# Differential attention on one core: the second map's weights scaled and added by one VectorE operation per unit, instead of two GpSimd operations

## The chip, the core and the metric

The kernel runs on one core of a Trainium2 chip. The metric is the device time of one execution in microseconds (us); the time of before is the median of three runs. The engines have short names in the profile: PE is TensorE (PEld is its loading of weights), DVE is VectorE, ACT is ScalarE, POOL is GpSimd, SP is the engine that issues the DMAs.

## The reference

Two layers over 1024 tokens of width 1024: multi-head latent attention, then differential attention with a bias by distance. In the second layer every head has two softmax maps, and what multiplies the values is their weighted difference:

```python
sc = jnp.einsum('bqhcd,bkhcd->bhcqk', qb, k).astype(jnp.float32)
bias = -slopes[None, :, None, None, None] * dist[:, None, None]
p = jax.nn.softmax(sc + bias, axis=-1)
a = p[:, :, 0] - lam * p[:, :, 1]
return jnp.einsum('bhqk,bkhd->bqhd', a.astype(v.dtype), v)
```

All in float32; 8 heads of two 64-wide halves, 8 blocks of 128 queries each.

## The kernel before

The second layer's attention is cut into 64 units (`Unit1`), one for each head and block of 128 queries. Matrix products in float32 are made of three products of rounded parts (a high part `hi` and a remainder `lo`), so every operand is split in two before it is used.

One pass of the loop over `u` (from -1 to 64) starts unit `u + 1` and finishes unit `u`. All five engines run in the order in which the loop records their instructions; nothing is reordered in this part. What one pass does:

- PE: the scores of unit `u + 1` for both maps (L1277, 12 matmuls into two PSUM tiles `S`), the transposes of unit `u`'s combined weights `p` (L818, 8 of them into two PSUM tiles `T`), then 24 or 48 matmuls of a projection of the layer (L1155 to L1157, or L1148 to L1150 for `W` blocks), and in every odd pass the product of two units' weights with the values (L1312). In every even pass the output of that product is transposed (L1318), which takes a `T` tile too. When a head is complete, its normalised output is transposed in two `T` tiles (L1346, in the passes u = 13, 21, 29, 37, 45, 53 and 61; called a closing below).
- DVE: the maximum of map 0 and of map 1 (L1283, each with a small L1285 behind it), a remainder of the last projection block, the reciprocal and the ratio `l1` (L1295, L1296), the remainder of the split of the transposed weights (L826, twice), up to four steps of a head's normalisation (L1332, L113, L115, L117, and L1336, which scales 128x128 pieces of the output `o`), and the rounding of the next weight block (L99).
- ACT: the two exponentials (L1291), which leave the sums of their rows, the rounding of the transposed weights (L97), copies.
- POOL: the weighted sum of the two maps (`combine`, L1303 and L1304), and the remainder of the next weight block (L104, `wbl`).

`T` tiles are two, used in turn: a new transpose can only be written when the tile's last readers, L97 on ACT and L826 on DVE, are done. In the passes u = 48, 51, 54 and 57 (`DOUBLE`) two units are started, the second one behind the split. Pages of SBUF (`page`) come from one pool of 49.

Of the kernel before, what the change touches and what calls it, by code (L numbers as in the profile page):

```python
# [12 lines left out]
ALU = mybir.AluOpType  # L13
# [42 lines left out]
def body(tc, x, c, positions, ada_w, ada_b, norm_g, mla_w_in, mla_q_norm_g, mla_w_q_up,  # L56
# [4 lines left out]
    with ctx:  # L61
# [30 lines left out]
        V, A, G, T = nc.vector, nc.scalar, nc.gpsimd, nc.tensor  # L92
# [1167 lines left out]
        class Unit1:  # L1260
# [36 lines left out]

            def combine(self):
                p0, p1 = self.p
                if self.u in (0,):  # L1300
                    V.scalar_tensor_tensor(p0, p1, self.l1, p0, op0=ALU.mult, op1=ALU.add)
                else:
                    G.tensor_scalar(p1, p1, self.l1, 1.0, op0=ALU.mult, op1=ALU.mult)  # L1303
                    G.tensor_tensor(p0, p0, p1, op=ALU.add)  # L1304
                self.p = p0

        def pv1(acc, h, ch):
# [255 lines left out]
```

## Time and profile before

| | before |
|---|---|
| median of 3 runs | 1655.2 us (1653.62 to 1655.92) |
| profiled execution | 1657.92 us, span 1656.1 us |
| PE busy | 1541.9 us (93%) |
| DVE busy | 1192.3 us (72%) |
| ACT busy | 814.3 us (49%) |
| POOL busy | 752.8 us (45%) |
| mean granted TensorE clock | 0.978 |

The profiled execution is 1.8 us longer than its span (what lies around the first and the last instruction) and 2.7 us longer than the median. Busy times are sums over the whole kernel, whose stages have different limits: the latent attention lies at about 260 to 690 us, the differential attention at about 890 to 1530 us. A PE that reads as busy is not PE at its peak, since matmuls are pipelined and their ends are modelled.

### The profile page before, as it was taken

Reading aid. Unit: us, or ns where it says so; the run is one execution under the profiler, and the core shown is the slowest. Engines: PE = TensorE matmul, PEld = TensorE weight load, DVE = VectorE, ACT = ScalarE, POOL = GpSimd, SP = SyncE. Lnnn points to the kernel's source line nnn. Section 1 sums busy time; section 2 is a strip of 40 time slices with the busy share of each in tenths; the row PEclk is TensorE's granted clock in tenths of the full one; section 3 lists DMA queues with packets and bytes.
Section 4 is the critical chain, followed back from the end, with each engine's and each line's share of the span. In section 5 each row is a group of like instructions: output and inputs, shape, how many; then the busy total and the mean of one; then the engine's idle time right before and its main releaser. Section 6 shows DMA issues by size and latency. Waiting matters only on the chain. (4 is left out here: it accounts for less than half of the span.)

```text
span 1656.1 us, 24862 instructions
## 1 busy us (share of the span) xinstructions
PE 1541.9 (93%) x9111; PEld 1315.9 (79%) x9111; DVE 1192.3 (72%) x2189; ACT 814.3 (49%) x1614; POOL 752.8 (45%) x612
## 2 busy tenths in 40 slices
PE   4788999999999999999999999899999999999797
PEld 3787778888888888888787898788777887777686
DVE  6766666888888888885536558686867676766764
ACT  6422125776777777785223444444444444445411
POOL 4444472443453453573353544554545354544422
PEclk8899999999999999999999999999999999999899
DMA  9007662110211111211224122423141313125122
GB/s 365 20 14 239 205 212 78 40 40 15 64 34 47 51 40 52 81 62 39 102 89 153 64 90 77 153 77 106 61 128 64 103 51 128 53 89 191 64 73 92
DMA packets 91585, 153.31 MB, mean 93 GB/s; under 512 B 5872, under 2 KB 60230, under 8 KB 91464
## 3 DMA queue, kind: packets, MB, share of 16 engines
q1 hardware_dynamic: 91464, 151.73, 27.3%
q8 instruction: 72, 1.18, 0.3%
q14 instruction: 49, 0.40, 0.1%
HBM read 126.01 MB, written 25.17 MB: 91 GB/s over the span
## 5 line engine op out<-in xcount | busy, mean ns | idle before, releaser
L826 DVE TENSOR_TENSOR ptl<-T,pth 128x512 fp32r<-128x512 f32 x384 | 246.7, 684 | 48.1 <-ACT pth L97 43.8
L97 ACT ACTIVATE pth<-T 128x512 fp32r<-128x512 f32 x384 | 207.4, 591 | 93.0 <-PE T L818 87.9
L1283 DVE CUSTOM_DVE_ANT_0 p<-S,dist 128x1024 f32<-128x1024 f32 x128 | 156.2, 1220 | 130.7 <-PE S L1277 87.6
L1291 ACT ACTIVATE p<-p,m 128x1024 f32<-128x1024 f32 x128 | 147.5, 1153 | 157.0 <-DVE m L1285 141.1
L818 PE MATMUL T<-ident,p 128*128 128x128 f32 x1536 | 205.8, 276 | 12.9 <-POOL p L1304 5.5
L854 POOL TENSOR_SCALAR p<-p,l 128x1024 f32<-128x1024 f32 x128 | 144.2, 1126 | 152.0 <-DVE l L853 104.5
L818 PEld LDWEIGHTS T<-ident,p 128*128 128x128 f32 x1536 | 170.9, 141 | 50.8 <-POOL p L1304 15.8
L1303 POOL TENSOR_SCALAR p<-p,l 128x1024 f32<-128x1024 f32 x63 | 71.2, 1130 | 299.9 <-ACT pth L97 290.9
L1155 PE MATMUL A<-hT,wbh 128*128 128x512 f32 x416 | 167.4, 402 | 0.0
L1156 PE MATMUL A<-hT,wbh 128*128 128x512 f32 x416 | 163.2, 392 | 2.9 <-DVE hT L104 2.9
L1157 PE MATMUL A<-hT,wbl 128*128 128x512 f32 x416 | 162.8, 391 | 0.0
L1304 POOL TENSOR_TENSOR p<-p,p 128x1024 f32<-128x1024 f32 x63 | 158.4, 2515 | 5.3
L847 DVE TENSOR_REDUCE m<-S 128x1 f32<-128x1024 f32 x128 | 155.9, 1218 | 2.1 <-PE S L843 0.3
L852 ACT ACTIVATE p<-S,m 128x1024 f32<-128x1024 f32 x128 | 143.2, 1118 | 15.8 <-DVE m L847 10.4
L1277 PE MATMUL S<-KK,QQ 64*128 64x512 f32 x768 | 108.2, 408 | 5.1 <-DVE m L1283 5.1
L841 PE MATMUL S<-Kh,Q 96*128 96x512 f32 x256 | 108.4, 424 | 4.5 <-ACT p L852 2.6
L888 POOL TENSOR_TENSOR og<-ot,og 64x256 f32<-64x256 f32 x64 | 53.1, 830 | 130.6 <-DVE ot L887 128.5
L842 PE MATMUL S<-Kl,Q 96*128 96x512 f32 x256 | 100.4, 392 | 0.0
L843 PE MATMUL S<-Kh,Q 96*128 96x512 f32 x256 | 100.4, 392 | 0.0
L104 POOL TENSOR_TENSOR wbl<-wblk,wbh 128x1024 fp32r<-128x1024 f32 x32 | 78.0, 2440 | 36.9 <-issue 20.9
L1156 PEld LDWEIGHTS A<-hT,wbh 128*128 128x128 f32 x416 | 78.7, 189 | 18.6 <-DVE hT L104 3.7
L1155 PEld LDWEIGHTS A<-hT,wbh 128*128 128x128 f32 x416 | 78.6, 189 | 17.1 <-issue 1.3
(329 smaller groups left out, 3667.2 us busy)
## 6 DMA issues: line engine op xcount, KB each, us to landing
dist<-DD SPq DMA_DIRECT2D x64, 512.0 KB
adaw<-in_ada_w_dram SPq DMA_DIRECT2D x48, 512.0 KB
wblk<-in_diff_w_in_dram SPq DMA_DIRECT2D x32, 512.0 KB
qraw<-in_mla_w_q_up_dram SPq DMA_DIRECT2D x16, 288.0 KB
x<-in_x_dram SPq DMA_DIRECT2D x8, 512.0 KB
wraw<-in_mla_w_in_dram SPq DMA_DIRECT2D x8, 512.0 KB
OGD<-gt SPq DMA_DIRECT2D x8, 512.0 KB
Q<-RD SPq DMA_DIRECT2D x64, 64.0 KB
```

The source lines that it names most:

```text
L97: A.activation(o, i, AF.Copy)
L818: T.transpose(tp[:, i * P:(i + 1) * P], p[:, kt * P:(kt + 1) * P], ident)
L826: V.tensor_tensor(ptl[n][:, :, o], src, f(pth[n][:, :, o]), op=ALU.subtract)
L847: V.tensor_reduce(self.m, self.ps, axis=AX.XY, op=ALU.max, negate=True)
L852: A.activation(p.rearrange("p (a b) -> p a b", b=512), self.ps, AF.Exp, bias=self.m, accum_out=l)
L854: G.tensor_scalar(p, p, l, 1.0, op0=ALU.mult, op1=ALU.mult)
L1155: T.matmul(ps, w[0][:, k], a, start=k == 0, stop=False)
L1156: T.matmul(ps, w[0][:, k], b, start=False, stop=False)
L1157: T.matmul(ps, w[1][:, k], a, start=False, stop=k == 7)
L1283: V.tensor_tensor_reduce(out=p, in0=self.ps[c_].rearrange("p a b -> p (a b)"), in1=dist[self.u], op0=ALU.subtract, op1=ALU.max, scale=1.0, ...
L1291: A.activation(p, p, AF.Exp, bias=self.m[c_], scale=2.0 ** -(self.h + 1), accum_out=L0[self.h][:, self.qt:self.qt + 1] if c_ == 0 else sel ...
L1304: G.tensor_tensor(p0, p0, p1, op=ALU.add)
```

## The change

`combine` had two forms: for unit 0 one DVE instruction that multiplies `p1` by the column `l1` and adds `p0`, for the other 63 units two POOL instructions (scale `p1` in place, then add it to `p0`). The change uses the first form for all units.

```diff
             def combine(self):
                 p0, p1 = self.p
-                if self.u in (0,):
-                    V.scalar_tensor_tensor(p0, p1, self.l1, p0, op0=ALU.mult, op1=ALU.add)
-                else:
-                    G.tensor_scalar(p1, p1, self.l1, 1.0, op0=ALU.mult, op1=ALU.mult)
-                    G.tensor_tensor(p0, p0, p1, op=ALU.add)
+                V.scalar_tensor_tensor(p0, p1, self.l1, p0, op0=ALU.mult, op1=ALU.add)
                 self.p = p0
```

The orders of PE, ACT and SP stay what they were. From L1301 on the changed file's lines are numbered 4 lower.

DVE in the pass u = 21, a closing (the time 1116 to 1125 us in the trace of before): `S` are the scores, `l` is `l1`, `ptl` the remainder of the transposed weights, `o` the head's output. Before:

```order
L1283 ISA p_11469,m_2170_11468<-S_11438,dist_11230 128x1024
L1283 ISA m_2170_11468 128x1
L1285 TENSOR_SCALAR m_2170_11468<-m_2170_11468 128x1
L1174 SCALAR_TENSOR_TENSOR QQ_11451<-A_11395,QQ_11451 128x512
L1295 RECIPROCAL l_2172_11472<-l_2172_11472 128x1
L1296 SCALAR_TENSOR_TENSOR l_2172_11472<-l_2052_10832,nlam,l_2172_11472 128x1
L826 TENSOR_TENSOR ptl_11388<-T_11458,pth_11387 128x4x128
L826 TENSOR_TENSOR ptl_11392<-T_11463,pth_11391 128x4x128
L1336 TENSOR_SCALAR o_9970<-o_9970,ory_11099 128x128 x4
```

And now, at the same place:

```order
L1283 ISA p_11448,m_2170_11447<-S_11417,dist_11211 128x1024
L1283 ISA m_2170_11447 128x1
L1285 TENSOR_SCALAR m_2170_11447<-m_2170_11447 128x1
L1174 SCALAR_TENSOR_TENSOR QQ_11430<-A_11374,QQ_11430 128x512
L1295 RECIPROCAL l_2172_11451<-l_2172_11451 128x1
L1296 SCALAR_TENSOR_TENSOR l_2172_11451<-l_2052_10817,nlam,l_2172_11451 128x1
L1300 SCALAR_TENSOR_TENSOR p_11433<-p_11448,l_2172_11451,p_11433 128x1024
L826 TENSOR_TENSOR ptl_11367<-T_11437,pth_11366 128x4x128
L826 TENSOR_TENSOR ptl_11371<-T_11442,pth_11370 128x4x128
L1332 TENSOR_SCALAR o_9963<-o_9963,ory_11081 128x128 x4
```

The new instruction for unit 22 (L1300) stands between the ratio and the two splits of unit 21 (L826), so the splits and everything behind them on DVE come after it; L1336 of before is L1332 now.

POOL over the passes around u = 16 to 20, where `wbl` is the remainder of a weight block. Before:

```order
L1303 TENSOR_SCALAR p_11057<-p_11057,l_2096_11060 128x1024
L1304 TENSOR_TENSOR p_11042<-p_11042,p_11057 128x1024
L104 TENSOR_TENSOR wbl_11105<-wblk_10935,wbh_11104 128x1024
L1303 TENSOR_SCALAR p_11174<-p_11174,l_2118_11177 128x1024
L1304 TENSOR_TENSOR p_11159<-p_11159,p_11174 128x1024
L1303 TENSOR_SCALAR p_11263<-p_11263,l_2135_11266 128x1024
L1304 TENSOR_TENSOR p_11248<-p_11248,p_11263 128x1024
L104 TENSOR_TENSOR wbl_11307<-wblk_11135,wbh_11306 128x1024
L104 TENSOR_TENSOR wbl_11311<-wblk_11137,wbh_11310 128x1024
```

And now:

```order
L104 TENSOR_TENSOR wbl_11087<-wblk_10919,wbh_11086 128x1024
L104 TENSOR_TENSOR wbl_11287<-wblk_11117,wbh_11286 128x1024
L104 TENSOR_TENSOR wbl_11291<-wblk_11119,wbh_11290 128x1024
```

Of POOL's work in this stage only the remainders of weight blocks are left.

## Rows read from the trace of the kernel before

**Rows 1.** Busy time of each engine in the stretch of the differential attention: us from the span's start, its length, busy us and instructions of each engine, then granted clock, DMA share and GB/s.

```profile
890.00:1530.00 640.00, 614.32 (x3821) 512.24 (x3819) 445.73 (x910) 294.79 (x630) 299.86 (x155) 0.99 0.29 95
```

**Rows 2.** The waits of PE, of its weight loads and of DVE in the same stretch: who waited for whom, us in total, times, the longest.

```profile
PE T L1346 <- DVE o L1336: 12.1, 9, 2.0
PE T L818 <- POOL p L1304: 5.5, 6, 1.2
PE S L1277 <- DVE m L1283: 5.1, 8, 0.9
...
PEld T L818 <- POOL p L1304: 15.8, 23, 1.6
...
DVE p L1283 <- PE S L1277: 87.6, 34, 5.6
```

**Rows 3.** POOL's groups of instructions in the same stretch: shapes and count, busy us, mean ns of one, then the idle time before them.

```profile
L1304 POOL TENSOR_TENSOR p<-p,p 128x1024 f32<-128x1024 f32 x63 | 158.4, 2515 | 5.3
L1303 POOL TENSOR_SCALAR p<-p,l 128x1024 f32<-128x1024 f32 x63 | 71.2, 1130 | 299.9 <-ACT pth L97 290.9 <-DVE l L1296 2.4 <-PE T L1185 2.2
L104 POOL TENSOR_TENSOR wbl<-wblk,wbh 128x1024 fp32r<-128x1024 f32 x29 | 70.5, 2434 | 36.2 <-issue 20.9 <-DVE wbh L99 10.8 <-PE A L1312 4.5
```

**Rows 4.** DVE's groups in the same stretch, in the same form.

```profile
L1336 DVE TENSOR_SCALAR o<-o,ory 128x128 f32<-128x128 f32 x48 | 25.1, 584 | 0.2
...
L113 DVE TENSOR_TENSOR ort<-ory 128x8 f32<-128x8 f32 x19 | 18.3, 963 | 0.4
L117 DVE SCALAR_TENSOR_TENSOR ory<-ort,ory 128x8 f32<-128x8 f32 x19 | 16.9, 888 | 0.7
...
L1332 DVE SCALAR_TENSOR_TENSOR oms<-oms,oss 128x8 f32<-128x8 f32 x7 | 13.9, 1984 | 0.2
L115 DVE SCALAR_TENSOR_TENSOR ort<-ort,oms 128x8 f32<-128x8 f32 x19 | 12.0, 629 | 0.5
```

**Rows 5.** Two of these lines over the whole kernel: shortest, median and longest duration in ns, first and last start.

```profile
L1336 DVE TENSOR_SCALAR o<-o,ory x64: 273/279/2429, 1030.6 to 1580.0; 128x128 f32<-128x128 f32 x64
...
L1332 DVE SCALAR_TENSOR_TENSOR oms<-oms,oss x8: 166/2278/2307, 998.0 to 1576.2; 128x8 f32<-128x8 f32 x8
```

**Rows 6.** A closing, u = 21, in order of time for DVE, POOL and PE: start us, duration us, engine, line, count, and in brackets the idle time before with its releaser.

```profile
1120.94 1.29 DVE L826 TENSOR_TENSOR ptl<-T,pth 128x512 fp32r<-128x512 f32 x2
1122.14 2.96 DVE L1336 TENSOR_SCALAR o<-o,ory 128x128 f32<-128x128 f32 x4
...
1122.29 2.34 POOL L1304 TENSOR_TENSOR p<-p,p 128x1024 f32<-128x1024 f32 x1
...
1121.68 0.66 PE L1346 MATMUL T<-ident,o 128*128 128x128 f32 x4 [0.17 <-DVE ptl L826]
1122.57 0.30 PE L1346 MATMUL T<-ident,o 128*128 128x128 f32 x1 [0.23 <-DVE o L1336]
1124.77 0.90 PE L1346 MATMUL T<-ident,o 128*128 128x128 f32 x3 [1.90 <-DVE o L1336]
1125.32 3.27 PE L1312 MATMUL A<-pth,V 128*128 128x256 f32 x16
```

**Rows 7.** Four stretches of 4 us behind closings, in the columns of rows 1.

```profile
1124.00:1128.00 4.00, 3.23 (x16) 3.21 (x17) 2.40 (x5) 0.00 (x0) 0.63 (x1) 0.57 0.19 80
1208.00:1212.00 4.00, 2.69 (x13) 2.57 (x14) 3.49 (x6) 0.00 (x0) 1.55 (x2) 0.72 0.09 35
...
1376.00:1380.00 4.00, 2.97 (x14) 2.94 (x15) 3.26 (x6) 0.00 (x0) 1.50 (x2) 0.63 0.13 55
...
1468.00:1472.00 4.00, 3.86 (x21) 3.75 (x22) 2.27 (x6) 0.00 (x0) 1.59 (x2) 0.65 0.46 148
```

**Rows 8.** Unit 0's combination, the one that DVE makes already, with what stands around it on DVE.

```profile
899.32 0.22 DVE L1296 SCALAR_TENSOR_TENSOR l<-l,nlam,l 128x1 f32<-128x1 f32 x1
899.58 1.28 DVE L1301 SCALAR_TENSOR_TENSOR p<-p,l,p 128x1024 f32<-128x1024 f32 x1
900.78 0.68 DVE L99 CAST wbh<-wblk 128x1024 fp32r<-128x1024 f32 x1
```

**Rows 9.** Splits (for one of them with the ratio ahead of it) and output transposes of three even passes, DVE's rows and then PE's: the first of the stage, the one with the widest and the one with the narrowest distance.

```profile
928.99 1.29 DVE L826 TENSOR_TENSOR ptl<-T,pth 128x512 fp32r<-128x512 f32 x2
...
987.57 0.22 DVE L1296 SCALAR_TENSOR_TENSOR l<-l,nlam,l 128x1 f32<-128x1 f32 x1
987.86 1.29 DVE L826 TENSOR_TENSOR ptl<-T,pth 128x512 fp32r<-128x512 f32 x2
1110.77 1.29 DVE L826 TENSOR_TENSOR ptl<-T,pth 128x512 fp32r<-128x512 f32 x2
...
930.68 0.38 PE L1318 MATMUL T<-ident,ot 128*128 128x128 f32 x2
989.90 0.38 PE L1318 MATMUL T<-ident,ot 128*128 128x128 f32 x2
1112.18 0.38 PE L1318 MATMUL T<-ident,ot 128*128 128x128 f32 x2
```

**Rows 10.** The pass with two weight-block remainders that came closest to the next ratio: DVE's rounding, POOL's remainders, DVE's next ratio.

```profile
1104.90 1.29 DVE L99 CAST wbh<-wblk 128x1024 fp32r<-128x1024 f32 x2
...
1105.66 5.14 POOL L104 TENSOR_TENSOR wbl<-wblk,wbh 128x1024 fp32r<-128x1024 f32 x2 [1.11 <-DVE wbh L99]
...
1110.41 0.41 DVE L1296 SCALAR_TENSOR_TENSOR l<-l,nlam,l 128x1 f32<-128x1 f32 x1
```

## The prediction, made before the changed kernel was run

> **What bounds the kernel now.** I read the busy times of the whole span first (the table above: PE 93%, DVE 72%, POOL 45%), then those of the stretch in which the change lies, 890 to 1530 us: PE is busy 614.3 of 640 us, DVE 445.7, POOL 299.9 [rows 1]. So this stage is PE's, and all that the change can give back directly are PE's 25.7 idle us and the time that PE spends at a lower clock. Next the waits of PE in that stretch [rows 2]: 12.1 us at the closings of heads (L1346 waits for the scaled pieces of `o`, L1336), 5.5 us at the transposes L818 for POOL's L1304, 5.1 us at the second scores of the passes that start two units. The weight loads show the second of these as 15.8 us in 23 waits, but most of that lies beside a matmul that is still running.
>
> Then I asked why L1336 is late. It takes 273 ns at its shortest and 279 in the middle, yet 2429 at its longest [rows 5], and in the closing at 1122 us four of them take 2.96 us: the group starts at 1122.14, POOL's L1304 runs from 1122.29 to 1124.63, and PE goes on at 1124.77 [rows 6]. The tiny steps of the normalisation do the same: L1332 works on 8 columns, takes 166 ns at its best and 2278 in the middle [rows 5]. So a DVE instruction that meets a running L1304 stands still until it ends. Busy time minus count times the undisturbed duration (0.279 for L1336, 0.17 for the others) is 11.7 us for L1336, 15.1 for L113, 13.7 for L117, 12.7 for L1332 and 8.8 for L115, together 62 us of DVE that reads as busy and is standing still [rows 4].
>
> The Trainium skill has a rule for this, on the page "SBUF — State Buffer", section "Who interferes with whom": VectorE and GpSimd share a pair of ports as an exclusive lock, which a VectorE instruction needs in a two-port mode, or with two SBUF inputs against a GpSimd instruction that reads SBUF, and who comes second is held for the whole of the other. The standstills agree with it. By that rule the instruction that the change adds can be held in the same way, by what POOL still does; its price is in rival 2.
>
> **The change, part by part.** Removed: 63 times L1303 and L1304, 229.6 us of POOL [rows 3]. That in itself is worth nothing, since POOL is idle half the stage. Added: 63 DVE instructions of the form that unit 0 uses already: 1.28 us, with the next one starting 1.20 us after it [rows 8]. DVE in the stage goes from 445.7 to 445.7 + 63 x 1.28 - up to 62, some 465 us of 625: 74%, still not the bound. Five things then move PE, (a) to (e).
>
> On the Trainium skill's page "Perfetto Trace Analysis", section "Optimizing Scalar/DVE Operations", one finds that work of a saturated VectorE may be handed to other engines, even to GpSimd; the change does the opposite. If DVE were the bound here, the time would be that of rival 3 in place of the sum below; 445.7 of 640 us speaks against it, and the page itself adds that the shared port can undo such a move.
>
> (a) The transposes no longer wait for POOL. The weights were ready 3.6 us behind the ratio (1.13 + 2.5 [rows 3]), now 1.24 us. In the passes where they waited, the scores stand between, 1.6 us of PE work. The gain is 5.5 us by PE's row; it counts only what lies behind the modelled end of the matmul before. The loads' row, 15.8, counts what lies beside that matmul too, and is the upper bound. PE's row is the nearer; I take 7, a little above it.
>
> (b) The closings. Six lie in the stage. There, L1336 would find POOL idle. Between the second split and the last piece there then remain four times some 0.22 us, and L1346 of the second tile must follow these; on the other side the splits come 1.17 us later, which the pass before gives back, since its own standstill of about 2.1 us [rows 5] is gone too. I put the rest at 0.5 us a closing, between 0.3 (only the pieces) and 1.4 (the whole of the late split besides): 12.1 - 6 x 0.5 = 9 us gained, between 3.7 and 10.3.
>
> (c) The clock. Behind four of the six closings the granted clock falls from 1.00 to between 0.57 and 0.72 over 4 us, behind a wait of PE of 1.9 us [rows 6, 7]; in part of these stretches PE runs at 1.2 GHz in place of 2.4. The matmuls of L1312 then take 3.27 us for 16. Time lost: 4 us x (0.43 + 0.28 + 0.37 + 0.35) = 5.7 us. PE's waits of 1.2 us at L818 [rows 2] have no such dip behind them in any slice I read. If a closing costs 0.5 us, all four dips go: 5.7 us; if it keeps 1.4, perhaps none.
>
> (d) The price. L826 starts 1.17 us later in each pass (the new instruction starts 0.04 us behind the ratio's end and occupies 1.20 [rows 8]; L826 started 0.07 behind it, as at 987.57 + 0.22 to 987.86 [rows 9]). The transposes of `p` hold both `T` tiles until L826 has read them. In even passes L1318 is the next to want one. From the end of the first L826 (0.68 us after the pair's start) to L1318 there are 1.01 us in the first such pass, 1.36 in the widest and 0.73 in the narrowest; read the same way, 20 of the 27 lie between 0.9 and 1.15, and three more passes, with a transpose of values there instead, at 1.0 to 1.1 [rows 9]. From a release to PE's start it takes 0.06 us (1120.94 + 0.68 to 1121.68 in [rows 6]). So PE stands 1.17 + 0.06 - 1.01 = 0.22 us where it did not, nothing in the widest, 0.50 in the narrowest: 0.17 in the mean, 30 x 0.17 = 5 us lost, between 0 (if DVE starts its maxima earlier) and 30 x 0.5 = 15. In odd passes the `T` tiles are wanted only by the next pass, closings apart.
>
> (e) The passes that start two units get two combinations, and the second unit's maxima lie behind the first one's. The scores that wait there (5.1 us) wait for the first unit's maxima, which stand ahead of any combination, so this wait stays. The pass behind starts up to 1 us late on DVE; four times, a third of it reaching PE: 1.5 us lost, between 0 and 4 x 1.2.
>
> What else reads the moved work has time: the product L1312 takes the split parts at the end of odd passes, its high parts first (the low parts' turn comes 16 matmuls behind 1125.32, and the split began at 1120.94 [rows 6]), and POOL's remainders, which start earlier now, belong to a block that PE takes up later.
>
> Sum: -7 - 9 - 5.7 + 5 + 1.5 = -15.2 us. Against the profiled execution: 1657.9 - 15.2 = 1642.7 (its span 1656.1 plus 1.8 around it). That execution was 2.7 us above the median, so I forecast 1655.2 - 15.2 = **1640 us**.
>
> **The rivals.**
>
> 1. *The closing's wait only changes its cause* (late splits in place of standstills). Each closing keeps 1.4 us, the clock dips stay: -7 - 3.7 + 5 + 1.5 = -4.2, 1651 us. For it: L1346 already waits 0.17 us for L826 before its other waits [rows 6], so a later split is felt in full. Against it: DVE's standstill in the pass before is longer than the delay.
>
> 2. *The combination meets the remainders of weight blocks and is held by them; slower.* There are 29 of L104 in the stage, 2.43 us each [rows 3]. One that starts just ahead of a combination would delay it and L826 by up to 2.4 us, and in an even pass PE by 2.4 + 0.2 us. Six such meetings use up the forecast gain (15.2 / 2.4 = 6.3); at 12 of them the time is 1655 + 14 = 1669. Against it: a remainder starts 0.8 us after its rounding began, the rounding is DVE's last work in a pass, and two maxima and two exponentials, over 4 us, lie between it and the next ratio. Even the pair that came closest was through at 1110.80, with the ratio at 1110.82 [rows 10].
>
> 3. *DVE becomes the bound; slower.* In 34 passes DVE waits for the scores before its first maximum, 87.6 us in all [rows 2]; in the other 30 it does not. If each of those passed 1.2 us on to PE, 36 us would be lost, in place of (d), against 20.2 from the other terms: 1655.2 + 15.8 = 1671. It decides from 0.7 us a pass. Against it: DVE loses about as much standstill (62) as it gains work (81), and idle time is left in two passes of three.
>
> 4. *It gives more than that*: the splits aren't felt (0 in place of 5), and a dip at 1437 us, behind the waits of a pass with two units, goes as well, for 1.7 us as behind a closing: 1640 - 5 - 1.7 = 1633.
>
> That the scheduler undoes the change isn't possible here, as the order is written out; that all of it is hidden would need PE's waits for POOL and L1336 to have other causes, 1655 us.
>
> **How the numbers follow.** Forecast, with its own range 1633 to 1648: 0.66. Rival 4: 0.09. Rival 1: 0.11, half of it within 0.2% of before, which is 3.3 us and about what a measurement can tell from no change. Rival 2: 0.07; rival 3: 0.04. No effect: 0.03. Faster: 0.66 + 0.09 + 0.05 = 0.80; same: 0.06 + 0.03 = 0.09; slower 0.11. The range for 8 in 10 leaves out the slower rivals and the far end of rival 4: 1630 to 1654.
>
> **What the profile after would show.** L1300 64 times at 1.28 us; if its mean is over 1.5, rival 2 has begun. L1332 (L1336 before) near 0.28 and the small steps near 0.17 us; if they stay long, the standstill had another cause. PE's wait for POOL at L818 gone; the wait at the closings 3 us in all, not 12; a new wait of PE at L1314 (L1318 before) for L826, 4 to 6 us in some 25 times. The stage's length 625 us, clock 1.00 behind the closings. I am wrong if PE waits more than 15 us for L826, or if the first maximum no longer starts with the end of the scores in even passes.

## The result and the profile after

The changed kernel takes 1637.6 us (median, 1636.5 to 1641.0) against 1654.5 beside it: ratio 0.9901, 95% interval [0.9887, 0.9915], 16.9 us faster. The forecast was 1640 us, 15.2 faster. On another chip (e7 below) the ratio was 0.9896 [0.9881, 0.9911]. The profiled execution has a span of 1639.1 us.

The stage can be measured without its neighbours, from the start of the first maximum (L1283) to that of the last: 894.0 to 1522.6 us before, 895.7 to 1505.2 after, so 628.6 and 609.5 us: 19.1 us less. The whole gained 2 us less than the stage, nearly all of it because the stage began 1.7 us later in this execution; in the runs below it begins between 891.6 and 896.1 us, whatever the kernel. I therefore give stage lengths beside the ratios. Each is read from one profiled execution, so differences of 1 or 2 us between them mean little.

The page's busy times, and the stretch of the stage (us from the start, length, busy us and instructions of PE, PEld, DVE, ACT, POOL, then granted clock, DMA share, GB/s; to be held against [rows 1]):

```profile
PE 1536.8 (94%) x9111; PEld 1304.1 (80%) x9111; DVE 1197.1 (73%) x2252; ACT 812.7 (50%) x1614; POOL 522.1 (32%) x486
...
890.00:1513.00 623.00, 612.62 (x3825) 504.65 (x3826) 451.18 (x975) 294.50 (x630) 70.13 (x29) 1.00 0.30 98
```

POOL lost 230 us of work and DVE's busy time rose by 5 only. The reason is in DVE's lines of the stage (line, shapes, count, busy us, mean ns, idle before; to be held against [rows 4]):

```profile
L1300 DVE SCALAR_TENSOR_TENSOR p<-p,l,p 128x1024 f32<-128x1024 f32 x64 | 82.2, 1285 | 2.2
...
L1332 DVE TENSOR_SCALAR o<-o,ory 128x128 f32<-128x128 f32 x48 | 10.4, 280 | 0.2
...
L117 DVE SCALAR_TENSOR_TENSOR ory<-ort,ory 128x8 f32<-128x8 f32 x19 | 3.2, 167 | 0.6
L113 DVE TENSOR_TENSOR ort<-ory 128x8 f32<-128x8 f32 x19 | 3.1, 163 | 0.4
L115 DVE SCALAR_TENSOR_TENSOR ort<-ort,oms 128x8 f32<-128x8 f32 x19 | 3.1, 163 | 0.4
...
L1328 DVE SCALAR_TENSOR_TENSOR oms<-oms,oss 128x8 f32<-128x8 f32 x7 | 1.2, 167 | 0.2
```

The pieces of `o` went from 584 to 280 ns in the mean, the step on 8 columns (L1332 before, L1328 now) from 1984 to 167: the standstill is gone. PE's waits in the stage, then its weight loads' and DVE's (to be held against [rows 2]):

```profile
PE S L1277 <- DVE m L1283: 4.5, 8, 0.8
PE T L1342 <- DVE o L1332: 1.4, 6, 0.2
...
PE T L1342 <- DVE ptl L826: 0.7, 2, 0.5
...
PEld T L1314 <- DVE ptl L826: 9.3, 21, 0.5
...
DVE p L1283 <- PE S L1277: 101.5, 49, 4.3
```

The 12.1 us at the closings are 2.1 now, the 5.5 us for POOL have no line any more, and a new wait has come: the output transposes' loads wait for the splits, 21 times. DVE waits for scores more often than before (49 passes, not 34). The closing of [rows 6], the same place now, DVE's rows and then PE's:

```profile
1118.63 1.28 DVE L1300 SCALAR_TENSOR_TENSOR p<-p,l,p 128x1024 f32<-128x1024 f32 x1
1119.83 1.28 DVE L826 TENSOR_TENSOR ptl<-T,pth 128x512 fp32r<-128x512 f32 x2
1121.03 0.86 DVE L1332 TENSOR_SCALAR o<-o,ory 128x128 f32<-128x128 f32 x4
...
1120.57 0.65 PE L1342 MATMUL T<-ident,o 128*128 128x128 f32 x4 [0.49 <-DVE ptl L826]
1121.45 0.82 PE L1342 MATMUL T<-ident,o 128*128 128x128 f32 x4 [0.23 <-DVE o L1332]
1122.03 2.15 PE L1308 MATMUL A<-pth,V 128*128 128x256 f32 x16
```

From the closing's first transpose to the product it takes 1.46 us, where it took 3.64; and the product's 16 matmuls take 2.15 us, not 3.27. The granted clock behind this closing, in 4 us slices, stays at 1.00, where [rows 7] had 0.57:

```profile
1120.00:1124.00 4.00, 3.28 (x25) 2.88 (x25) 3.09 (x8) 0.66 (x2) 0.00 (x0) 1.00 0.02 8
1124.00:1128.00 4.00, 4.00 (x34) 3.33 (x33) 1.23 (x2) 0.38 (x1) 0.00 (x0) 1.00 1.02 297
```

Read in such slices from the first maximum to the last, the stage lost 8.5 us to a lower clock before (slice length times what is missing to 1.00) and loses nothing now.

### The profile page after: what moved, and what is told of

Same layout as the page of the kernel before. It is cut to its first block, busy times and chain, and to the rows that moved or that the text cites. A ratio compares the mean times of both kernels' runs of the same rounds, so it can differ in the third digit from the quotient of the medians.

```text
span 1639.1 us, 24613 instructions
## 1 busy us (share of the span) xinstructions
PE 1536.8 (94%) x9111; PEld 1304.1 (80%) x9111; DVE 1197.1 (73%) x2252; ACT 812.7 (50%) x1614; POOL 522.1 (32%) x486
## 5 line engine op out<-in xcount | busy, mean ns | idle before, releaser
L826 DVE TENSOR_TENSOR ptl<-T,pth 128x512 fp32r<-128x512 f32 x384 | 246.2, 682 | 45.8 <-ACT pth L97 45.7
L1283 DVE CUSTOM_DVE_ANT_0 p<-S,dist 128x1024 f32<-128x1024 f32 x128 | 156.1, 1219 | 111.7 <-PE S L1277 101.5
L854 POOL TENSOR_SCALAR p<-p,l 128x1024 f32<-128x1024 f32 x128 | 143.7, 1122 | 151.9 <-DVE l L853 104.5
L852 ACT ACTIVATE p<-S,m 128x1024 f32<-128x1024 f32 x128 | 143.1, 1118 | 15.8 <-DVE m L847 10.4
L1157 PEld LDWEIGHTS A<-hT,wbl 128*128 128x128 f32 x416 | 78.2, 188 | 16.8
L1277 PEld LDWEIGHTS S<-KK,QQ 64*128 64x128 f32 x768 | 67.8, 184 | 28.2 <-DVE m L1283 6.7
```

Of the source, the lines that this page charges most:

```text
L826: V.tensor_tensor(ptl[n][:, :, o], src, f(pth[n][:, :, o]), op=ALU.subtract)
L852: A.activation(p.rearrange("p (a b) -> p a b", b=512), self.ps, AF.Exp, bias=self.m, accum_out=l)
L854: G.tensor_scalar(p, p, l, 1.0, op0=ALU.mult, op1=ALU.mult)
L1157: T.matmul(ps, w[1][:, k], a, start=False, stop=k == 7)
L1277: T.matmul(self.ps[c_][:, n], q[r, zq, sl], k[zk][r, n * 512:(n + 1) * 512], start=i == 0, stop=i == 2)
L1283: V.tensor_tensor_reduce(out=p, in0=self.ps[c_].rearrange("p a b -> p (a b)"), in1=dist[self.u], op0=ALU.subtract, op1=ALU.max, scale=1.0, ...
```

## The experiments

Two theories stood against each other on where the gain lies: in the closings, because VectorE no longer stands still beside GpSimd, with the clock dips behind them; or in the transposes, which no longer wait for GpSimd's result. A third question was the price: do the later splits cost what I said?

**e1, splits ahead of the combination.** The new instruction stays on VectorE, but behind L826:

```diff
                     nx.ratio()
-                    nx.combine()
                 if cur:
                     chunks[u // 2].split(units[u], tps)
+                for nx in nxs[:1]:
+                    nx.combine()
```

> As the changed kernel, but VectorE's combination is recorded behind the two splits of the unit before (ratio, L826 twice, combination) in place of ahead of them; in the passes that start two units only the first unit's is moved. Theory (the price of the change is the T tiles that stay held while the splits stand behind the combination): the splits come 1.2 us earlier, the waits of the weight loads for L826 at the output transposes (9.3 us in 21) go, and some 5 us of the time with them: 1633 us, ratio to the kernel before 0.987. Rival (those waits lie beside running matmuls and cost nothing): 1637.6, the time of the changed kernel. Second rival (the weights come 1.2 us too late for the transposes): slower than 1640, with a wait of L818 for the combination.

Measured: 0.9862 [0.9845, 0.9878], 1634.6 us beside 1657.3; the stage is 604.8 us, 4.7 shorter than with the change. Waits of PE in the stage:

```profile
PE S L1277 <- DVE m L1283: 4.5, 8, 0.8
PE T L1342 <- DVE o L1332: 3.9, 6, 1.2
```

In the stage no output transpose waits for L826, and none of the unit's transposes for the weights, which come 1.2 us later. The price was real. The closings' wait for the pieces of `o` has grown from 1.4 to 3.9, since they now come behind the combination.

**e2, GpSimd's load given back, without anyone waiting for it.**

```diff
                 V.scalar_tensor_tensor(p0, p1, self.l1, p0, op0=ALU.mult, op1=ALU.add)
+                if self.u > 0:
+                    G.tensor_scalar(p1, p1, self.l1, 1.0, op0=ALU.mult, op1=ALU.mult)
+                    G.tensor_tensor(p1, p1, p1, op=ALU.add)
```

> As the changed kernel, with GpSimd given back its two instructions for units 1 to 63 (a scaling and an addition of 128x1024, reading SBUF), now on the dead weights of map 1 behind VectorE's combination; nobody uses their result. It puts back the load of GpSimd without the dependence. Theory (the gain came from VectorE no longer standing still while GpSimd runs): the small steps of the normalisation are up to 2.4 us long again and the scaled pieces L1332 meet the addition, so that the closings wait 2 us each again and the clock dips come back: 1637.6 + 6 x 2 + 4 to 6 x 1.7 = 1656 to 1660 us. Rival (the gain came from PE no longer waiting for GpSimd's result): 1638 us, since no one waits for GpSimd here.

Measured: 1.0100 [1.0077, 1.0123], 1675.4 us; stage 644.9 us, 35 longer than with the change. DVE's lines and PE's waits (numbers are 3 higher here than in the changed kernel, so L1335 are the pieces, L1331 the step on 8 columns, L1345 and L1317 the transposes):

```profile
L1335 DVE TENSOR_SCALAR o<-o,ory 128x128 f32<-128x128 f32 x48 | 29.4, 674 | 0.2
...
L1331 DVE SCALAR_TENSOR_TENSOR oms<-oms,oss 128x8 f32<-128x8 f32 x7 | 11.4, 1627 | 0.2
...
PE T L1345 <- DVE o L1335: 10.4, 12, 1.5
PE T L1345 <- DVE ptl L826: 8.4, 6, 2.1
PE T L1317 <- DVE ptl L826: 5.3, 6, 2.1
```

With nobody waiting for GpSimd the closings' waits are back, and larger. The sign is the theory's; the size was 1656 to 1660 and came out 15 us above, because GpSimd starts behind the combination here and ends later: a standstill at the end of one pass makes the next one's splits late too (8.4 and 5.3 us), and the slices lose 15.4 us to the clock. So e2 shows what standing still can do; it does not give the size of what the change removed.

**e3, twice the work on VectorE.**

```diff
                 V.scalar_tensor_tensor(p0, p1, self.l1, p0, op0=ALU.mult, op1=ALU.add)
+                V.scalar_tensor_tensor(p1, p1, self.l1, p1, op0=ALU.mult, op1=ALU.add)
```

> As the changed kernel, with a second VectorE instruction of the same form and size behind each combination, on weights that are dead by then. Theory (in even passes each 1.2 us more ahead of the split is 1.2 us more of PE, since the distance is used up; odd passes still have 3 to 4 us): 27 + 3 passes x 1.2 + 6 closings x 1.2 = 43 us more, 1680 us. Rival (VectorE has room, 451 of 623 us busy, and an instruction of 1.2 us finds idle time): at most 10 us more, below 1648. Rival (VectorE is near its bound in every pass): 64 x 1.2 = 77 us more, 1715.

Measured: 1.0251 [1.023, 1.0273], 1698.8 us; stage 671.5 us, 62 longer.

PE's waits (numbers are 1 higher here than in the changed kernel):

```profile
PE T L1315 <- DVE ptl L826: 37.9, 27, 3.4
PE T L1343 <- DVE ptl L826: 7.4, 6, 1.8
```

The waits came where the theory has them, 27 output transposes at 1.4 us (the 1.2 added and the 0.2 that were there) and 6 closings at 1.2. What I left out is the clock again: the slices up to the last maximum lose 12 us. So behind the splits PE pays for each further us, but only in half of the passes; VectorE as such isn't the bound.

**e4 and e5, half of the units each.** In e4 the combination is on VectorE only for units whose pass has normalisation steps; in e5 only for the others (the bracket behind `or` negated). The diff is e4's:

```diff
                 p0, p1 = self.p
-                V.scalar_tensor_tensor(p0, p1, self.l1, p0, op0=ALU.mult, op1=ALU.add)
+                if self.u == 0 or (self.u > 9 and (self.u - 1) % 8 in (1, 2, 3, 4, 5)):
+                    V.scalar_tensor_tensor(p0, p1, self.l1, p0, op0=ALU.mult, op1=ALU.add)
+                else:
+                    G.tensor_scalar(p1, p1, self.l1, 1.0, op0=ALU.mult, op1=ALU.mult)
+                    G.tensor_tensor(p0, p0, p1, op=ALU.add)
```

> The combination on VectorE only for the units that are combined in the passes in which a head's normalisation steps run on VectorE (five of eight passes from u = 9 on); in the others GpSimd's two instructions as in the kernel before. Theory (the closings and their clock dips carry most of the gain): closings -10, clock -6, price of the splits +2 (13 of the even passes), of the waits for GpSimd's weights only 0.5 of 5.5 gained: -14.5 from 1654.5, 1640 us. Rival (the waits of the transposes for GpSimd carry it): 5 of those 5.5 us are in the other passes, so 1654 to 1656 us, no gain.

Measured for e4: 0.9909 [0.9891, 0.9928], stage 613.1 us. Its waits:

```profile
PE T L818 <- POOL p L1304: 4.9, 6, 1.0
...
PE T L1346 <- DVE o L1336: 3.0, 6, 1.9
```

> The other half of the units: the combination on VectorE only for units that are combined outside the passes with normalisation steps (three of eight passes from u = 9 on, and all before); GpSimd's two instructions in the rest. Theory (closings and clock carry the gain): the waits for GpSimd's weights go for the most part (-5), the splits cost +2.5, closings and clock dips stay as before: ratio 0.998 to 1.000, hardly faster. Rival (the gain lies in the transposes' waits): ratio 0.992 to 0.994, more than half of the change's gain.

Measured for e5: 0.9957 [0.9941, 0.9974], stage 622.9 us. Its waits:

```profile
PE T L1346 <- DVE o L1336: 10.2, 8, 2.0
...
PE T L818 <- POOL p L1304: 0.5, 1, 0.5
```

With 35 of the 63 combinations moved, e4 has the change's gain within the intervals, and still pays nearly all of the waits for GpSimd (4.9 of 5.5 us). Of its 3.0 us at closings one wait of 1.9 is the sixth closing, whose unit lies outside my rule of eight, since the passes that start two units shift the count. e5 shows the other part: PE waits 5.0 us less for GpSimd (the loads 15.8 - 5.4 us less), 1.9 less at closings, and loses 1.6 less to the clock; against these 8.5 us stand 4.4 us of new load waits at the output transposes, of which some part reaches PE. The stage gained 5.7 us, the ratio says 7. Its expectation of hardly any gain was too low, and the rival's too high. The two halves' gains (15 and 7 us) add up to more than the whole (17); with intervals of some 3 us each I leave that open.

**e6, GpSimd busy without reading.** Four fills in place of e2's two instructions:

```diff
                 V.scalar_tensor_tensor(p0, p1, self.l1, p0, op0=ALU.mult, op1=ALU.add)
+                if self.u > 0:
+                    for _ in range(4):
+                        G.memset(p1, 0.0)
```

> As the changed kernel, with four fills of the dead weights of map 1 (128x1024 each) on GpSimd behind each combination of units 1 to 63: GpSimd is busy beside VectorE again but reads nothing. If VectorE stands still only beside a GpSimd instruction that reads SBUF, as the Trainium skill's page SBUF — State Buffer, section Who interferes with whom, has it for VectorE instructions with two SBUF inputs, then the small steps stay at 0.17 us, and only what runs in a two-port mode (L1332 in its new number, L99) may be held: 1638 to 1655 us scaled, ratio 0.990 to 1.000. If any running GpSimd instruction holds VectorE, the small steps are as long as in the run that reads: ratio 1.00 to 1.01.

Measured: 1.0005 [0.9996, 1.0014], stage 626.8 us. The time lies where the two expected ranges meet and decides nothing; the durations do. GpSimd's fills, and DVE's lines (numbers as in e2):

```profile
L1303 POOL MEMSET p<- 128x1024 f32 x251 | 251.0, 1000 | 302.9 <-DVE p L1300 217.2 <-ACT pth L97 47.8 <-PE A L1157 9.4
...
L99 DVE CAST wbh<-wblk 128x1024 fp32r<-128x1024 f32 x29 | 30.0, 1042 | 0.0
L1335 DVE TENSOR_SCALAR o<-o,ory 128x128 f32<-128x128 f32 x48 | 23.8, 899 | 0.2
...
L110 DVE TENSOR_SCALAR ory<-ory 128x8 int32<-128x8 int32 x7 | 7.1, 1008 | 0.0
...
L117 DVE SCALAR_TENSOR_TENSOR ory<-ort,ory 128x8 f32<-128x8 f32 x19 | 3.2, 167 | 0.7
...
L1331 DVE SCALAR_TENSOR_TENSOR oms<-oms,oss 128x8 f32<-128x8 f32 x7 | 1.2, 167 | 0.2
```

Although GpSimd ran 251 us beside VectorE, the steps with two SBUF inputs stayed at 167 ns, and 63 of these 64 steps ran beside a fill; the pieces of `o` and the roundings, which have one input, were held (280 to 899 and 685 to 1042 ns), and so was a step of the same 8 columns with one input (L110, 162 to 1008 ns). The time is back at that of before because the held pieces, and splits that come late behind them, made PE wait 9.3 and 5.1 us at the closings. This is the Trainium skill's rule in "SBUF — State Buffer", section "Who interferes with whom": two SBUF inputs contend only with a GpSimd instruction that reads SBUF, a two-port copy or scaling with either. The trace agrees with it.

**e7, the changed kernel again.**

> The changed kernel once more, to have it beside the others on this chip. Both theories: ratio 0.990.

Measured: 0.9896 [0.9881, 0.9911], stage 609.4 us.

**e8, e9, e10: the closings cleared by order.** One number makes the last pieces of `o` one pass earlier, so that no closing waits for them:

```diff
-                pump(fin, 4)
+                pump(fin, 5)
```

e8 has this and e1's order, e9 has it alone in the kernel before (combination on GpSimd), e10 in the changed kernel.

> The kernel with the splits ahead of the combination, and with five normalisation steps in a pass in place of four, so that all eighteen are done one pass ahead of the closing. Theory (what is left at a closing is the pieces of L1332 behind the combination, 3.9 us in six waits): these waits go, closings take only the T tiles, 4 to 6 us less than the kernel with the splits first: ratio 0.983. Rival (the extra step makes even passes late and PE waits there): ratio 0.986 or above, with new waits of the output transposes for L826.

> The kernel before, GpSimd's combination and all, with five normalisation steps in a pass in place of four, so that the last scaled pieces are made one pass ahead of the closing. Theory (of the standstills only those in a closing pass reach PE; elsewhere VectorE has the time): the 12.1 us of closings go, and the clock dips behind them (6.8 of 8.5), while GpSimd's 5.5 us at the transposes stay: ratio 0.988 to 0.990, about the change's own gain, with VectorE's small steps still up to 2.4 us. Rival (the standstill only moves and makes the pass ahead of the closing late): ratio 0.995 or above, with waits of PE for L826 or for the maxima in its place.

> The changed kernel with five normalisation steps in a pass, splits still behind the combination: it parts the two edits of the kernel that has both (ratio 0.982). Theory: the closings' rest goes (2.1 us of matmul waits and some of the loads'), the waits of the output transposes for L826 stay at 9 us and those of the closings grow: ratio 0.986 to 0.988. Rival (the splits do not matter, and the extra step does all): 0.982.

Measured: e8 0.9816 [0.9801, 0.983], 1624.6 us, stage 598.7; e9 0.9869 [0.984, 0.9899], stage 608.5; e10 0.9857 [0.9831, 0.9882], stage 606.5. PE's largest waits in e8:

```profile
PE S L1277 <- DVE m L1283: 4.5, 8, 0.8
PE T L818 <- ACT junk L1318: 1.1, 2, 0.7
```

In e9, PE's waits and DVE's lines:

```profile
PE T L818 <- POOL p L1304: 5.4, 6, 1.2
PE S L1277 <- DVE m L1283: 5.3, 8, 0.9
...
L1336 DVE TENSOR_SCALAR o<-o,ory 128x128 f32<-128x128 f32 x48 | 25.3, 587 | 0.2
...
L115 DVE SCALAR_TENSOR_TENSOR ort<-ort,oms 128x8 f32<-128x8 f32 x20 | 21.5, 1075 | 0.7
L1332 DVE SCALAR_TENSOR_TENSOR oms<-oms,oss 128x8 f32<-128x8 f32 x7 | 13.9, 1986 | 0.2
```

And in e10:

```profile
PEld T L1314 <- DVE ptl L826: 9.3, 21, 0.5
...
PEld T L1342 <- DVE ptl L826: 3.6, 11, 0.7
```

e9 is the sharpest of all: VectorE stands still as much as before, the pieces at 587 ns, the step on 8 columns at 1986, and yet the kernel is as fast as the changed one or faster, since no closing waits for it; the slices lose 1.7 us to the clock, not 8.5. These 1.7 us (1420 to 1428 us) lie in the second of the passes that start two units, with a standstill of 2.34 us (L115 at 1415.38) shortly ahead of its first maximum. So standstill cost something at the six closings and in this one pass. Once the closings are cleared, moving the combination is worth 2 us of stage (608.5 to 606.5) as the change writes it, ratios that the intervals don't part, and 10 us with the splits first (598.7): 5.4 us of waits for GpSimd then go without the price coming. e8 is the fastest kernel of the study, 13 us below the changed one by the ratios (0.9816 and 0.9896 on the same chip).

## Why the prediction was right

The time came out 2.4 us below the forecast, and the likeliest case was the one that happened; the stage itself gained 4 us more than the sum said. By its terms:

(a) *Waits for GpSimd, 7 us.* PE's 5.5 us are gone, and e5, which takes away little else, gained 6 to 7 us with about 3.5 from closings and clock in it, less the price of its splits. Right, and not finer than a few us.

(b) *Closings, 9 us.* 12.1 went to 1.4 + 0.7, 10.0 us. The rest was put at 0.5 a closing; it is 0.35 by PE's rows. The step "the pass before gives the delay back" held: in the closing shown PE waits 0.49 us for L826, where it waited 0.17.

(c) *Clock, 5.7 us: too small.* It was 8.5. I had read one slice behind each closing, and the dip reaches into the next one; and there was a dip at no closing at all, behind the second scores of a pass that starts two units, which I left to rival 4:

```profile
1436.00:1440.00 4.00, 3.11 (x15) 1.90 (x15) 3.10 (x8) 3.42 (x6) 0.72 (x1) 0.81 0.00 2
1440.00:1444.00 4.00, 4.00 (x15) 3.23 (x14) 3.04 (x7) 2.10 (x3) 2.79 (x2) 0.77 0.01 4
```

These are slices of the kernel before, 1.7 us lost. After the change that pass's first maximum starts 0.03 us behind the end of the scores, where it was 0.46, because the standstill ahead of it is gone: PE's two waits there are 0.30 and 0.84 us instead of 0.72 and 0.89, and no slice is below 1.00. In e9, where the standstill ahead of that maximum stays, the waits are 0.92 and 0.89 and the dip stays too. That waits of 1.2 us leave no dip held for GpSimd's waits here, but not in e3: there two closings with waits of 1.28 and 1.32 us had slices at 0.57 and 0.82 behind them, and one of 1.52 us had none.

(d) *Later splits, 5 us.* From the end of the scores to the output transpose it took 6.36 us in most even passes (as in [rows 9]'s first, 924.32 to 930.68) and takes 6.49 to 6.62, and the scores behind it start 0.06 later: 0.2 a pass. e1 returned 4.7 us of stage although its closings lost 2.5, so with closings and the transposes of values the whole price is about 7. The new wait stands in the loads' row (9.3 us), not in PE's, where I had expected it; by 0.2 us in each of 27 passes about half of it was time.

(e) *Passes that start two units, 1.5 us: not there.* Their waits fell from 5.1 to 4.5 us. The pass behind was late on VectorE by about 1 us, as said, but only twice (its first maximum 0.92 and 1.14 us behind the scores' end), and PE's rows show two waits of 0.3 us there.

With these measured sizes the sum is -5.5 - 10 - 8.5 - 0.6 + 5 = -19.6, or -17.6 with e1's 7 for the splits; the stage's is -19.1. The errors did not cancel: the clock, sized 2.8 us too small, (b), 1.0 too small, and (e), 2.1 too large, all made the forecast too slow, and only (a) took back 1.5 of it. The whole came nearer to the forecast than the stage because the stage began later in that execution, which is luck.

Of the rivals, the second falls with L1300 itself, 1.283 to 1.289 us in all 64: no combination met a remainder of a weight block. (The pair in [rows 10] was closer than I read it: 1110.82 is the ratio's end, and it took 0.41 us for its usual 0.22, so it had been held.) The third falls with the 49 waits for scores. The first was wrong for the changed kernel, but e1 shows how near it lay: with the pieces 1.2 us later the closings cost 3.9.

What I did not ask was whether the standstill mattered anywhere but at the closings. I computed 62 us of it and showed that it reached PE in six closings; the conclusion that another order of VectorE's own steps would do as much as the whole change was open to me, and e9 made it.

## What to carry to other kernels

Hold the shortest duration of an instruction against its mean: the small one here with a mean of ten times its best was standing still, and its neighbour in time on the other engine was what held it; then ask in which passes that reaches the engine that bounds the kernel, since those few passes can be cleared by order alone. When work is put on an in-order engine, its price is not its duration but the distance between the next release behind it and the one who wants it: put the new work behind the release, not ahead of it. A wait of the matmul engine costs its length, and may cost nearly as much again through the clock behind it: here 1.7 us behind four of the six waits of 1.9 us, nothing behind the other two.

## What the runs showed of the hardware

GpSimd that only fills memory holds VectorE's copies and scalings with one input (899 and 1042 ns in the mean, for 280 and 685), and leaves instructions with two SBUF inputs alone (167 ns); GpSimd that reads holds both (674 and 1627 ns for the pieces and the step on 8 columns in e2). The clock's share was larger than expected: in e2 and e3, where PE waits 24 and 45 us for pieces and splits at the transposes, another 15 and 12 us went in slices below 1.00, down to 0.50 over 4 us, the lower of the two levels.
